# Two transformer blocks on one core: the first weights k-tile by k-tile behind idle products, transposes inside a product, the last tokens tile by tile

## The chip, the core and the metric

One NeuronCore of a Trainium2 chip runs the whole program; the other cores do nothing. The metric is the device time of one execution in microseconds (us), median of 3 runs. TensorE (PE in the profile) multiplies, VectorE (DVE) and ScalarE (ACT) do elementwise work, GpSimd (POOL) a few small operations, SyncE (SP) issues nearly all loads from memory.

## What is computed

256 tokens of width 1024 pass through two blocks. Only the skeleton matters here:

```python
def first_block(x, ...):
    x = x + 0.5 * swiglu(rms_norm(x, ffn1_norm), w_gate, w_up, w_down)        # FFN 1
    x = x + concat(attention(...), pooled(...)) @ w_out                       # first mixer
    x = x + 0.5 * swiglu(rms_norm(x, ffn2_norm), w_gate, w_up, w_down)        # FFN 2

def second_block(x, ...):
    x = x + 0.5 * swiglu_2(rmsnorm(x, ffn1_norm), ...)                        # FFN 3
    x = x + hybrid_mixer(rmsnorm(x, mix_norm), ...)                           # second mixer
    x = x + 0.5 * swiglu_2(rmsnorm(x, ffn2_norm), ...)                        # FFN 4
    return rmsnorm(x, final_norm)
```

`swiglu(h) = (silu(h @ w_gate) * (h @ w_up)) @ w_down`, with 2816 hidden columns. `rms_norm` divides each token by the root of its mean square and multiplies by a gain for each column.

## The kernel before, in words

The tokens are two tiles of 128 (t = 0, 1), kept as `X[t]` (128 x 1024, float32). A product that has to be nearly exact in float32 is made of three products of float32r operands: each operand is split into a high part and a remainder (`split`, lines 63 to 65: ACT copies to `whi`, DVE subtracts to `wlo`), and `mm3` (lines 67 to 72) adds high x high, high x remainder and remainder x high. So 128 tokens times one k-tile (128 rows of a weight) times 512 columns are three PE instructions of 512 columns, on lines 70, 71 and 72.

Weights come in chunks of 128 x 2048 float32 (1 MB), four k-tiles of 512 columns each, through `weights` (lines 53 to 61): a load on SP into one of 3 buffers `raw`, then the two halves of the split into one of 4 buffers `whi` and `wlo`. `rows` (line 94) multiplies a chunk with both token tiles: 24 PE instructions. `feed` (lines 120 to 124) makes the other operand: a k-tile of the transposed tokens times the gain of the norm, split into two parts in `hT`. The norm's division comes later, as a scale `r` from `rstd` (squares by `squares` on ACT, a sum on DVE, a power on POOL).

Each FFN (`ffn`, line 199) works through six column blocks j of gate (G) and up (U); `gated` takes silu(G) on ACT and multiplies with U on DVE, and the transposes of that result are put into `self.late` and done by a `flush` inside a later product. Then two column halves f of the down product (`d`, five chunks of 1 MB and one of 0.5 MB each) are added to X by `add` (line 151), which also takes the squares and, where a norm follows, puts the transposes of X with their `feed` into `self.late` (`pair`).

The start is special: nothing is on the chip yet. `cold_start` (line 178) loads the first chunk of G in four pieces of 256 KB, a piece and its k-tile of the transposed input `xT` at a time, and multiplies it piece by piece: 24 products. The other three chunks of block j = 0 (U, then G, then U again: 72 products) come whole through `weights`, and the tokens `X` themselves are loaded between them.

The first mixer ends with `project` (line 470): four products of mixed tokens with chunks of `w_out`, each for a half of the input and a half f of the columns. The last one is `project(0, 1)`; behind its 24 products `flush` gives PE the transposes of the left half of X, which the first product of FFN 2 needs.

After FFN 4, `run` multiplies X with the last gain, computes `r`, scales on ACT and DVE, and stores four pieces of 256 KB from SP.

The program is written through a tile framework that places the semaphores and, by a model of its own, sets the order of instructions within each engine. Each engine then runs its list in that order.

## Time and profile before

| | us |
|---|---|
| median of 3 runs | 1105.01 |
| lowest, highest | 1104.85, 1106.17 |
| profiled execution: device time | 1106.03 |
| profiled execution: span of the trace | 1104.2 |
| PE busy | 1083.4 |
| DVE busy | 608.8 |
| ACT busy | 506.9 |
| POOL busy | 13.7 |

The profiled execution is 1.0 us slower than the median of the runs, and its own time is 1.8 us more than its span. Times in the trace count from the start of the span. PE is busy nearly all the time, by a modelled end of each pipelined instruction: what PE loses shows as idle time before an instruction, or as a longer distance between the starts of two instructions.

### The profile page before, as it was taken

The page shows a single profiled execution, that of the slowest core. Times are in us where ns is not written, and L with a number is a line of the kernel's source. Part 1 is how long each engine was busy: PE and PEld are TensorE (multiplying, and loading weights), DVE is VectorE, ACT ScalarE, POOL GpSimd, SP SyncE. Part 2 cuts the span into 40 slices and gives each one's busy share as a digit, 9 for nine tenths or more (in the row PEclk, how much of TensorE's full clock was granted, in tenths as well). Part 3 has the DMA queues.
Part 4 walks back from the last instruction along what each step waited for, and adds up shares of the span by engine and source line. Part 5 has one row for each costly group of instructions (what it writes and reads, how often), then busy time and mean ns, then how long its engine had stood idle before and what let it go on. Part 6 is the DMA issues. An engine that isn't in the chain of part 4 may idle for free.

```text
span 1104.2 us, 12761 instructions
## 1 busy us (share of the span) xinstructions
PE 1083.4 (98%) x5250; PEld 907.2 (82%) x5250; DVE 608.8 (55%) x649; ACT 506.9 (46%) x588; POOL 13.7 (1%) x27
## 2 busy tenths in 40 slices
PE   6999999999999999999999999999999999999996
PEld 4888888878788888888888888999888888888885
DVE  4655545698555455445555455687545465545551
ACT  5544434578444444444444444534444345444431
POOL 0000000020000000000000000000000000000000
PEclk8999999999999999999999999999999999999999
DMA  8765544634345554565555455454555555555431
GB/s 305 281 227 191 191 168 150 218 124 171 114 175 191 191 177 174 184 216 211 183 191 191 172 177 200 176 191 157 187 190 191 181 178 178 187 191 187 172 137 39
DMA packets 31739, 201.76 MB, mean 183 GB/s; under 512 B 4545, under 2 KB 4929, under 8 KB 8769
## 3 DMA queue, kind: packets, MB, share of 16 engines
q1 hardware_dynamic: 31680, 200.95, 51.5%
q8 instruction: 41, 0.67, 0.2%
q14 instruction: 18, 0.14, 0.0%
HBM read 199.88 MB, written 1.05 MB: 182 GB/s over the span
## 4 chain that ended last, share of the span: by engine, by line
PE 79%; issue 17%; ACT 1%; DMA 1%; DVE 1%; SPq 0%; POOLq 0%; POOL 0%; ACTq 0%
PE ps L70 25%; PE ps L71 25%; PE ps L72 25%; PE ps L78 2%; PE ps L111 2%; DMA raw<-in_gu 1%; ACT whi L64 1%; DVE wlo L65 1%; PE ps L171 1%; ACT ro L372 0%; PE ps L488 0%; SPq L190 0%; PE ps L384 0%; ACT junk L130 0%; PE ps L318 0%
## 5 line engine op out<-in xcount | busy, mean ns | idle before, releaser
L65 DVE TENSOR_TENSOR wlo<-raw,whi 128x2048 fp32r<-128x2048 f32 (+2 forms) x193 | 425.6, 2206 | 394.4 <-ACT whi L64 394.2
L64 ACT ACTIVATE whi<-raw 128x2048 fp32r<-128x2048 f32 (+2 forms) x193 | 356.1, 1846 | 434.4 <-PE ps L72 315.6
L70 PE MATMUL ps<-whi,hT 128*128 128x512 f32 (+1 forms) x912 | 358.9, 394 | 10.0 <-ACT whi L64 8.5
L71 PE MATMUL ps<-wlo,hT 128*128 128x512 f32 (+1 forms) x912 | 356.0, 390 | 1.6 <-DVE wlo L65 1.6
L72 PE MATMUL ps<-whi,hT 128*128 128x512 f32 (+1 forms) x912 | 355.5, 390 | 0.0
L70 PEld LDWEIGHTS ps<-whi,hT 128*128 128x128 f32 x912 | 172.4, 189 | 45.5 <-ACT whi L64 8.9
L71 PEld LDWEIGHTS ps<-wlo,hT 128*128 128x128 f32 x912 | 172.6, 189 | 36.7 <-DVE wlo L65 2.5
L72 PEld LDWEIGHTS ps<-whi,hT 128*128 128x128 f32 x912 | 172.3, 189 | 35.7
L70 PE MATMUL ps<-whi,act 128*128 128x512 f32 x352 | 138.6, 394 | 0.0
L72 PE MATMUL ps<-whi,act 128*128 128x512 f32 x352 | 138.1, 392 | 0.0
L71 PE MATMUL ps<-wlo,act 128*128 128x512 f32 x352 | 138.0, 392 | 0.0
L72 PEld LDWEIGHTS ps<-whi,act 128*128 128x128 f32 x352 | 66.1, 188 | 14.9
L71 PEld LDWEIGHTS ps<-wlo,act 128*128 128x128 f32 x352 | 66.2, 188 | 14.5
L70 PEld LDWEIGHTS ps<-whi,act 128*128 128x128 f32 x352 | 66.1, 188 | 14.5
L211 ACT ACTIVATE sg<-ps,rstd 128x512 f32<-128x512 f32 (+1 forms) x48 | 31.4, 654 | 64.4 <-PE ps L72 49.5
L70 PE MATMUL ps<-hT,whi 128*128 128x256 f32 x192 | 54.4, 283 | 0.0
L71 PE MATMUL ps<-hT,whi 128*128 128x256 f32 x192 | 54.3, 283 | 0.0
L72 PE MATMUL ps<-hT,wlo 128*128 128x256 f32 x192 | 54.3, 283 | 0.0
L157 DVE SCALAR_TENSOR_TENSOR X<-ps,X 128x512 f32<-128x512 f32 x28 | 19.2, 689 | 44.1 <-PE ps L72 44.1
L213 DVE SCALAR_TENSOR_TENSOR pr<-ps,rstd,sg 128x512 f32<-128x512 f32 (+1 forms) x48 | 33.7, 704 | 12.7 <-PE ps L72 8.5
L71 PEld LDWEIGHTS ps<-hT,whi 128*128 128x128 f32 x192 | 36.9, 192 | 0.0
L70 PEld LDWEIGHTS ps<-hT,whi 128*128 128x128 f32 x192 | 36.9, 192 | 0.0
(152 smaller groups left out, 693.5 us busy)
## 6 DMA issues: line engine op xcount, KB each, us to landing
raw<-in_gu SPq DMA_DIRECT2D x87, 1024.0 KB, 4.8
raw<-in_d SPq DMA_DIRECT2D x40, 1024.0 KB, 4.7
raw<-in_w_out SPq DMA_DIRECT2D x8, 1024.0 KB, 5.0
raw<-in_w_cx SPq DMA_DIRECT2D x8, 1024.0 KB, 4.9
raw<-in_w_v SPq DMA_DIRECT2D x6, 1024.0 KB, 4.9
raw<-in_w_u SPq DMA_DIRECT2D x6, 1024.0 KB, 4.9
raw<-in_de SPq DMA_DIRECT2D x8, 512.0 KB, 3.5
raw<-in_w_b SPq DMA_DIRECT2D x4, 1024.0 KB, 4.9
```

The source lines that it names most:

```text
L64: self.nc.scalar.activation(hi, x, AF.Copy)
L65: self.nc.vector.tensor_tensor(lo, x, hi.bitcast(F32), op=ALU.subtract)
L70: mm(ps, lhsT=a[0], rhs=b[0], start=start, stop=False)
L71: mm(ps, lhsT=a[0], rhs=b[1], start=False, stop=False)
L72: mm(ps, lhsT=a[1], rhs=b[0], start=False, stop=stop)
L78: self.nc.tensor.matmul(ps, lhsT=a, rhs=b, start=start, stop=stop)
L111: self.nc.tensor.transpose(pt[:, i, :], x[t][:, i * P : i * P + P], self.ident)
L157: nc.vector.scalar_tensor_tensor(x, accs[t], scale, x, op0=ALU.mult, op1=ALU.add)
L171: nc.tensor.transpose(pt[:, i, t * P : t * P + P], self.X[t][:, (k + i) * P : (k + i) * P + P], self.ident)
L211: nc.scalar.activation(sg, gs[t], AF.Silu, scale=r[:, t : t + 1])
L213: nc.vector.scalar_tensor_tensor(pr, us[t], r[:, t : t + 1], sg, op0=ALU.mult, op1=ALU.mult)
```

## The change

It has three parts.

The start: `warm_up` gives PE 14 products of a tile of ones with itself, whose result nobody reads. `cold_start` now takes over the whole of block j = 0: all four chunks come in pieces of 256 KB. In the first half (c = 0) each k-tile of G is followed by that of U, in the second (c = 1) the four k-tiles of G come first, then `ident` and X are loaded, then the four of U. `xT` comes in four pieces of two k-tiles. Two loads, `gains` and the first piece of G, are issued by ACT instead of SP, ahead of the load of ACT's table.

```diff
+WARM = 14
...
-    def rows(self, accs, w, x, k0, nk, last, n=512):
+    def rows(self, accs, w, x, k0, nk, last, n=512, tiles=(0, 1)):
-        for t in range(2):
+        for t in tiles:
...
-    def add(self, accs, f, scale, following):
+    def add(self, accs, f, scale, following, tiles=(0, 1)):
-        for t in range(2):
+        for t in tiles:
             x = self.X[t][:, s]
...
-        for t in range(2):
+        for t in tiles:
             self.squares(t, f)
...
+    def warm_up(self):
+        ps = self.ps()
+        for _ in range(WARM):
+            self.mm(ps[:, :P], self.ones, self.ones)
+
     def cold_start(self, accs, src):
-        nc = self.nc
-        raw = self.raw.tile([P, 2048], F32, tag="raw", name="raw")
-        hi = self.wsp.tile([P, 2048], F32R, tag="whi", name="whi")
-        lo = self.wsp.tile([P, 2048], F32R, tag="wlo", name="wlo")
-        xT = self.raw.tile([P, KD, T], F32, tag="raw", name="xT")
+        nc, a = self.nc, self.a
         self.hT = self.big.tile([P, KD, 2, T], F32R, tag="hT", name="hT")
-        for k in range(4):
-            s = slice(k * 512, k * 512 + 512)
-            if k % 2 == 0:
-                nc.sync.dma_start(xT[:, k : k + 2, :], self.a["xT"][:, k : k + 2, :])
-            nc.sync.dma_start(raw[:, s], src[:, s])
-            self.feed(k, xT[:, k, :], "ffn1_norm")
-            self.split(hi[:, s], lo[:, s], raw[:, s])
-            for t in range(2):
-                self.mm3(accs[t], self.both(self.hT[:, k, :, t * P : t * P + P]), (hi[:, s], lo[:, s]), k == 0, False)
-        nc.sync.dma_start(xT[:, 4:8, :], self.a["xT"][:, 4:8, :])
-        for k in range(4, KD):
-            self.feed(k, xT[:, k, :], "ffn1_norm")
+        for c in range(2):
+            w = []
+            for i in range(2):
+                raw = self.raw.tile([P, 2048], F32, tag="raw", name="raw")
+                hi = self.wsp.tile([P, 2048], F32R, tag="whi", name="whi")
+                lo = self.wsp.tile([P, 2048], F32R, tag="wlo", name="wlo")
+                w.append((raw, hi, lo))
+            for i, k in [(i, k) for k in range(4) for i in range(2)] if c == 0 else [(i, k) for i in range(2) for k in range(4)]:
+                kd, s = 4 * c + k, slice(k * 512, k * 512 + 512)
+                raw, hi, lo = w[i]
+                if i == 0 and k % 2 == 0:
+                    xT = self.work.tile([P, 2, T], F32, tag="pr", name="xT", bufs=4)
+                    nc.sync.dma_start(xT, a["xT"][:, kd : kd + 2, :])
+                (nc.scalar if kd + i == 0 else nc.sync).dma_start(raw[:, s], src[i, c][:, s])
+                if kd + i == 0:
+                    first = self.small.tile([P, 1], F32, tag="tot1", name="first")
+                    nc.scalar.activation(first, self.ones[:, :1], AF.Silu)
+                if i == 0:
+                    self.feed(kd, xT[:, k % 2, :], "ffn1_norm")
+                self.split(hi[:, s], lo[:, s], raw[:, s])
+                for t in range(2):
+                    self.mm3(accs[i][t], self.both(self.hT[:, kd, :, t * P : t * P + P]), (hi[:, s], lo[:, s]), kd == 0, kd == KD - 1)
+                if c == 1 and i == 0 and k == 3:
+                    nc.sync.dma_start(self.ident, a["ident"])
+                    for t in range(2):
+                        nc.sync.dma_start(self.X[t], a["x"][t])
+        for t in range(2):
+            for f in range(2):
+                self.squares(t, f)
...
                 if j == 0 and first:
-                    self.cold_start(G, gu[0, 0])
-                else:
-                    self.token_major(G, gu[2 * j], 512, 0)
+                    self.cold_start((G, U), gu)
+                    r = self.rstd()
+                    gated(j, G, U)
+                    continue
+                self.token_major(G, gu[2 * j], 512, 0)
...
+            down = lambda f, c: self.weights(d[f, c] if c < 5 else d_end[f])
             for f in range(2):
                 accs = [self.ps() for _ in range(2)]
-                for c in range(6):
-                    self.rows(accs, self.weights(d[f, c] if c < 5 else d_end[f]), act, 4 * c, 4 if c < 5 else 2, KF - 1)
+                split = f == 1 and following == "final_norm_2"
+                for c in range(4 if split else 6):
+                    self.rows(accs, down(f, c), act, 4 * c, 4 if c < 5 else 2, KF - 1)
                     if c == 0:
                         self.flush()
-                self.add(accs, f, 0.5, following)
+                if split:
+                    ws = [down(f, c) for c in (4, 5)]
+                    for t in range(2):
+                        for c in (4, 5):
+                            self.rows(accs, ws[c - 4], act, 4 * c, 4 if c < 5 else 2, KF - 1, tiles=[t])
+                        self.add(accs, f, 0.5, following, [t])
+                else:
+                    self.add(accs, f, 0.5, following)
...
         def project(half, f):
             accs = [self.ps() for _ in range(2)]
             w = self.weights(a["w_out"][2 * half + f])
-            self.rows(accs, w, mT[half], 0, 4, 3)
-            self.flush()
+            for t in range(2):
+                self.rows(accs, w, mT[half], 0, 4, 3, tiles=[t])
+                self.flush()
             self.add(accs, f, 1.0, None if half else following)
...
-        first = self.small.tile([P, 1], F32, tag="tot1", name="first")
-        nc.scalar.activation(first, self.ones[:, :1], AF.Silu)
-        self.gains = self.load(self.const, "gains", [P, len(NORMS) * KD])
+        self.gains = self.const.tile([P, len(NORMS) * KD], F32, name="gains")
+        nc.scalar.dma_start(self.gains, a["gains"])
         self.ident = self.const.tile([P, P], F32, name="ident")
+        self.warm_up()
...
-        ys = []
-        both = self.raw.tile([P, 2, D], F32, tag="raw", name="y")
         for t in range(2):
-            y = both[:, t, :]
+            y = self.raw.tile([P, 2048], F32, tag="raw", name="y")[:, :D]
+            tot = self.small.tile([P, 1], F32, tag="tot1", name="tot")
+            nc.vector.tensor_tensor(tot, self.sq[:, 0, t : t + 1], self.sq[:, 1, t : t + 1], op=ALU.add)
+            r = self.small.tile([P, 1], F32, tag="r1", name="r1")
+            self.rsqrt(r, tot, 1.0 / D)
             for f in range(2):
                 s = slice(f * 512, f * 512 + 512)
                 nc.vector.tensor_tensor(y[:, s], self.X[t][:, s], self.fg[:, s], op=ALU.mult)
-            ys.append(y)
-        r = self.rstd()
-        for t in range(2):
             for f in range(2):
                 s = slice(f * 512, f * 512 + 512)
                 if f:
-                    nc.vector.tensor_scalar(ys[t][:, s], ys[t][:, s], r[:, t : t + 1], None, op0=ALU.mult)
+                    nc.vector.tensor_scalar(y[:, s], y[:, s], r, None, op0=ALU.mult)
                 else:
-                    nc.scalar.activation(ys[t][:, s], ys[t][:, s], AF.Copy, scale=r[:, t : t + 1])
-                nc.sync.dma_start(self.out[t * P : t * P + P, s], ys[t][:, s])
+                    nc.scalar.activation(y[:, s], y[:, s], AF.Copy, scale=r)
+                (nc.scalar if f == 0 and t == 1 else nc.sync).dma_start(self.out[t * P : t * P + P, s], y[:, s])
```

The first place is SP's list at the start. `xT` is the input, `raw` the weights' buffers (112 and 115 are G and U of the first half, 204 is G of the second), line 190 or 202 a piece, line 57 a whole chunk. Before:

```order
L665 DMA gains_84<-in_gains 128x56
L189 DMA xT_101<-in_xT 128x512
L190 DMA raw_98<-in_gu1 128x512 x2
L189 DMA xT_101<-in_xT 128x512
L190 DMA raw_98<-in_gu1 128x512 x2
L195 DMA xT_101<-in_xT 128x1024
L57 DMA raw_158<-in_gu1 128x2048
L57 DMA raw_188<-in_gu1 128x2048
L231 DMA ident_86<-in_ident 128x128
L233 DMA X0_82<-in_x 128x1024
L233 DMA X1_83<-in_x 128x1024
```
Now:

```order
L201 DMA xT_118<-in_xT 128x512
L202 DMA raw_115<-in_gu1 128x512
L202 DMA raw_112<-in_gu1 128x512
L202 DMA raw_115<-in_gu1 128x512
L201 DMA xT_162<-in_xT 128x512
L202 DMA raw_112<-in_gu1 128x512
L202 DMA raw_115<-in_gu1 128x512
L202 DMA raw_112<-in_gu1 128x512
L202 DMA raw_115<-in_gu1 128x512
L201 DMA xT_210<-in_xT 128x512
L202 DMA raw_204<-in_gu1 128x512 x2
```
`xT` has moved to the head of the list; `gains` and the first piece of G are gone from it, since ACT issues them. Behind these rows stand `ident`, both halves of X, four pieces of U, and from there on whole chunks. From SP's seventh load on each carries a wait for the landing of the load eight places before it (ACT's two counted), since the framework gives out eight completion semaphores in turn; the list of before has such waits too, with fewer and larger loads.

The second place is the end of the first mixer, on PE. `mT` is the mixed tokens, line 171 or 172 a transpose of a piece of X. Before (ps_2301 is the accumulator of the second token tile):

```order
L70 MATMUL ps_2301<-whi_2304,mT_2156 128x512
L71 MATMUL ps_2301<-wlo_2305,mT_2156 128x512
L72 MATMUL ps_2301<-whi_2304,mT_2156 128x512
L171 MATMUL ps_2332<-ident_86,X0_82 128x128
L171 MATMUL ps_2332<-ident_86,X1_83 128x128
```
Now (ps_2346 is the accumulator of the first token tile):

```order
L71 MATMUL ps_2346<-whi_2350,mT_2202 128x512
L72 MATMUL ps_2346<-wlo_2351,mT_2202 128x512
L73 MATMUL ps_2346<-whi_2350,mT_2202 128x512
L172 MATMUL ps_2366<-ident_84,X0_80 128x128
L172 MATMUL ps_2366<-ident_84,X1_81 128x128
```
The eight transposes have moved ahead of the last 12 products. On ACT, `feed` (line 123 or 124) turns their result into `hT`. Before:

```order
L64 ACTIVATE whi_2446<-raw_2444 128x2048
L130 ACTIVATE junk_2297,sq_2294<-X1_83 128x512
L130 ACTIVATE junk_2352,sq_2294<-X0_82 128x512
L64 ACTIVATE whi_2482<-raw_2480 128x2048
L123 ACTIVATE hT_2299<-ps_2332,gains_84 128x256
L123 ACTIVATE hT_2299<-ps_2341,gains_84 128x256
L130 ACTIVATE junk_2354,sq_2294<-X1_83 128x512
```
Now:

```order
L65 ACTIVATE whi_2492<-raw_2490 128x2048
L131 ACTIVATE junk_2343,sq_2340<-X1_81 128x512
L124 ACTIVATE hT_2345<-ps_2366,gains_82 128x256
L124 ACTIVATE hT_2345<-ps_2375,gains_82 128x256
L131 ACTIVATE junk_2398,sq_2340<-X0_80 128x512
L124 ACTIVATE hT_2345<-ps_2366,gains_82 128x256
L65 ACTIVATE whi_2528<-raw_2526 128x2048
L124 ACTIVATE hT_2345<-ps_2375,gains_82 128x256
L131 ACTIVATE junk_2400,sq_2340<-X1_81 128x512
```
Three of the four `feed` rows have moved ahead of the second split of a chunk; the fourth stands behind it.

The third place is DVE's list at the end (line 157 or 158 is `add`, 701 or 729 the product with the last gain, 708 or 733 the last scale). Before:

```order
L157 SCALAR_TENSOR_TENSOR X0_82<-ps_7713,X0_82 128x512
L701 TENSOR_TENSOR y_7890<-X0_82,fg_7148 128x512
L157 SCALAR_TENSOR_TENSOR X1_83<-ps_7714,X1_83 128x512
L701 TENSOR_TENSOR y_7890<-X1_83,fg_7148 128x512
L135 TENSOR_TENSOR tot_7895<-sq_7708 128x2
L84 TENSOR_SCALAR var_7898<-tot_7895 128x2
L708 TENSOR_SCALAR y_7890<-y_7890,rstd_7897 128x512 x2
```
Now:

```order
L158 SCALAR_TENSOR_TENSOR X0_80<-ps_7759,X0_80 128x512
L729 TENSOR_TENSOR y_7936<-X0_80,fg_7194 128x512
L724 TENSOR_TENSOR tot_7937<-sq_7754 128x1
L85 TENSOR_SCALAR var_7940<-tot_7937 128x1
L733 TENSOR_SCALAR y_7936<-y_7936,r1_7939 128x512
L158 SCALAR_TENSOR_TENSOR X1_81<-ps_7760,X1_81 128x512
L729 TENSOR_TENSOR y_7949<-X1_81,fg_7194 128x512
L724 TENSOR_TENSOR tot_7950<-sq_7754 128x1
L85 TENSOR_SCALAR var_7953<-tot_7950 128x1
L733 TENSOR_SCALAR y_7949<-y_7949,r1_7952 128x512
```
The first token tile's chain is complete before the second tile's `add`; on PE the last 18 products are now all of the second tile.

## Rows read from the trace of the kernel before

**Rows 1.** Part 1 of the page: busy time, share of the span, instructions of each engine.
```profile
PE 1083.4 (98%) x5250; PEld 907.2 (82%) x5250; DVE 608.8 (55%) x649; ACT 506.9 (46%) x588; POOL 13.7 (1%) x27
```

**Rows 2.** Waits of PE over the span: total us, times, longest us.
```profile
PE ps L70 <- ACT whi L64: 8.5, 2, 6.4
PE ps L71 <- DVE wlo L65: 1.6, 1, 1.6
PE ps L70 <- ACT hT L123: 1.5, 1, 1.5
```

**Rows 3.** PE by stretch: length, busy us (count), granted clock, DMA share, GB/s.
```profile
6.40:10.70 4.30, 4.29 (x9) 1.00 0.95 342
...
14.50:18.90 4.40, 0.73 (x2) 0.89 0.98 398
18.90:24.60 5.70, 5.67 (x13) 0.50 1.03 364
```

**Rows 4.** Timeline of the start: start us, us, engine, line, instructions.
```profile
0.73 0.20 POOL L675 MEMSET ones<- 128x128 f32 x1 [0.29 <-POOLq L801]
0.74 0.39 SPq L665 DMA_DIRECT2D gains<-in_gains  x1
...
1.18 0.42 SPq L189 DMA_DIRECT2D xT<-in_xT  x1
...
4.93 0.91 ACT L123 ACTIVATE hT<-xT,gains 128x256 fp32r<-128x256 f32 x2 [2.70 <-DMA xT<-in_xT]
...
5.75 1.14 ACT L64 ACTIVATE whi<-raw 128x512 fp32r<-128x512 f32 x2
...
6.41 0.79 PE L70 MATMUL ps<-whi,hT 128*128 128x512 f32 x1 [6.41 <-ACT whi L64]
...
7.14 0.79 PE L71 MATMUL ps<-wlo,hT 128*128 128x512 f32 x1
...
14.64 1.91 ACT L64 ACTIVATE whi<-raw 128x2048 fp32r<-128x2048 f32 x1 [0.75 <-DMA raw<-in_gu]
16.58 2.29 DVE L65 TENSOR_TENSOR wlo<-raw,whi 128x2048 fp32r<-128x2048 f32 x1 [2.17 <-ACT whi L64]
...
24.92 0.39 PE L71 MATMUL ps<-wlo,hT 128*128 128x512 f32 x1
...
43.10 1.03 PE L111 MATMUL ps<-ident,pr 128*128 128x128 f32 x8
```

**Rows 5.** DMA issues, 1.6 to 2.05 us: count, KB each, us to landing.
```profile
xT<-in_xT SPq DMA_DIRECT2D x1, 256.0 KB, 3.7
raw<-in_gu SPq DMA_DIRECT2D x1, 256.0 KB, 3.9
```

**Rows 6.** Timeline of PE at the second mixer's 128x128 f32 products.
```profile
780.87 1.95 PE L78 MATMUL ps<-gv,sgu_w 128*128 128x128 f32 x16
782.57 0.48 PE L70 MATMUL ps<-whi,hT 128*128 128x512 f32 x1
```

**Rows 7.** Timeline around the first mixer's end.
```profile
300.73 1.03 PE L171 MATMUL ps<-ident,X 128*128 128x128 f32 x8
300.93 1.91 ACT L64 ACTIVATE whi<-raw 128x2048 fp32r<-128x2048 f32 x1 [0.93 <-PE ps L72]
...
302.75 0.82 ACT L123 ACTIVATE hT<-ps,gains 128x256 fp32r<-128x256 f32 x2
...
303.26 0.50 PE L70 MATMUL ps<-whi,hT 128*128 128x512 f32 x1 [1.49 <-ACT hT L123]
```

**Rows 8.** Timeline of the end, and us from issue to landing of tile out.
```profile
1095.34 0.39 PE L72 MATMUL ps<-whi,act 128*128 128x512 f32 x1
...
1097.75 0.70 POOL L85 TENSOR_TENSOR rstd<-var,mhalf 128x2 f32<-128x2 f32 x1 [182.04 <-DVE var L84]
...
1098.99 1.81 SPq L711 DMA_DIRECT2D out<-y  x4
...
DMA to landing us min/median/max: 2.1/2.4/2.8
```

More of the change, by code (lines that the diff above doesn't have):

```diff
@@ L229, in ffn @@
                 if j == 0:
-                    if first:
-                        nc.sync.dma_start(self.ident, a["ident"])
-                        for t in range(2):
-                            nc.sync.dma_start(self.X[t], a["x"][t])
-                            for f in range(2):
-                                self.squares(t, f)
                     r = self.rstd()
@@ L701, in run @@
                 nc.vector.tensor_tensor(y[:, s], self.X[t][:, s], self.fg[:, s], op=ALU.mult)
-            ys.append(y)
-        r = self.rstd()
-        for t in range(2):
             for f in range(2):
```

## The prediction

> **What bounds the kernel now.** The first part of the page comes first: PE is busy for 1083.4 of 1104.2 us, every other engine for at most 609 [rows 1]. So only what PE loses can be won, and the list of what PE waits for says where: 8.5 and 1.6 us for the two halves of a weight's split, both within the first 19 us, and once 1.5 us for ACT's `hT` [rows 2]. The table by stretch then shows a loss that is no wait: from 18.9 to 24.6 us the granted clock is 0.50, the 1.2 GHz level, and 13 recorded products fill 5.67 us, 0.43 each [rows 3]. From 6.4 to 10.7 us nine recorded products fill 4.29 us, again at 0.43 or more; the column reads 1.00 there, but the distance is that of the lower level. The timeline gives the full pace: from 24.92 us to the first transposes at 43.10 lie 80 products, 0.227 us each [rows 4]. (Those transposes come after 120 products, the 96 of block j = 0 and 24 of the next, before and after the change alike; so their start measures the whole beginning.) The rest of the span runs at that pace, but for the 1.5 us at the first mixer's end and a tail after the last product.
>
> **The start: when the first products can run.** The first `xT` piece is SP's second load, issued at 1.18 us behind `gains` at 0.74; it takes 3.7 us to land, and ACT's `feed` starts at 4.93 [rows 4, 5]. Now it is SP's first, 0.44 us earlier: it lands at 4.45 and `feed`, 0.46 us (two take 0.91), ends at 5.0. The first piece of G goes out on ACT behind `gains`, at about 1.2 us (0.74 and one issue of 0.4); at 3.9 us to landing [rows 5] it is there at 5.1. Its high half takes 0.57 to 0.65 us (two take 1.14; the first product began 0.66 after the first split) and the first product runs at 5.8; the second needs DVE's remainder and came 0.73 us after the first [rows 4]: 6.5 us. ACT's table load, now behind two issues, is over by 3 us and stays under the wait for `xT`.
>
> From there PE does not wait if pieces come in time. A k-tile of both G and U is 12 products, 2.72 us. ACT needs one `feed` and two splits for it, 0.46 + 2 x 0.57 = 1.6 us, DVE about the same. Quarter splits are dearer than whole ones (4 x 0.57 = 2.28 against 1.91 us [rows 4]), some 1 us more on ACT in all, and that hides under PE as long as PE is the slower. SP issues a piece every 0.47 us, faster than any rate of landing seen. So product 120 is over at 6.5 + 119 x 0.227 = 33.5 us, against 43.10: **9.6 us**. About half of it is the clock (23 or so products at 0.2 us extra), the rest the waits at 14.6 to 18.9 us, where a whole chunk's split (1.91 on ACT, 2.29 on DVE) stood between landing and product.
>
> **The idle products.** They pay only for the clock. Eight products of this shape are 16 rows of the trace and take 1.70 us [rows 6], so 0.2125 each at full clock and 0.425 at half. They can begin at 1.0 us, after `ones` is set [rows 4]. Before, the full pace came 4.3 us after the first product (6.41 to 10.7) and 5.7 us after the second start (18.93 to 24.6) [rows 3, 4]. From 1.0 us that is 5.3 or 6.7 us: ten products at half clock and four at full end at 6.1, or all 14 end by 6.95. The real ones could start at 5.8 and are held by the second at 6.5, so the idle ones cost nothing or 0.45 us. I take **-0.1**, nearer to the first, since that row too starts from a cold chip. The Trainium skill (TensorE: Matmul & The Clock Gate, Part 1: The HAM clock gate) says that the point of release differs from run to run of the same kernel; by it the term would be 0 in some executions and -0.45 in others, which no run here can show yet.
>
> **The loads behind it.** What is late next is the first whole chunk, for j = 1. Up to its landing 7.4 MB must come: 1.05 of `xT`, 4.2 of pieces, 0.07 of `ident`, 1.05 of X, 1.05 of itself. With the queue full the rows show 342, 364 and 398 GB/s [rows 3]; at their mean, 368, the 7.14 MB after the first piece take 19.4 us and are there at 23.9. ACT's 1.91 and DVE's 2.29 bring 28.1, and PE wants the remainder at 6.5 + 96 x 0.227 = 28.3. At 398 there are 1.7 us to spare, at 342 it is 1.3 late. I take **-0.3**. Within the first block each piece has 3 to 4 us to spare at 368. X moves ahead of the last four pieces, and its squares ahead of their splits on ACT: about 3 us of ACT, done near 21 us, before the splits wanted at 22.8 us.
>
> **The first mixer's end.** Before, the transposes run at 300.73, but ACT has a chunk's split before the `feed` (300.93, 1.91 us), `feed` starts at 302.75, and PE waits 1.49 us until 303.26 [rows 7]. Now 12 products, 2.7 us, stand between the transposes and the first use, and three of four `feed` rows stand ahead of that split. X needs DVE's `add` of the product before, whose last instruction is now six products (1.4 us) ahead of the transposes; the `add` takes 0.7. The fourth `feed` still stands behind the split: 0.2 + 1.9 + 0.4 = 2.5 us after the last product of the mixer; the list has it used after 11 products of the next, also 2.5 us. Its remainder comes after DVE's next split, 4.9 us against 22 products, 5.0. So both just fit. Bounds: 1.5 if both do, 0.5 if one is a microsecond late; I take **1.4**.
>
> **The tail.** The last product starts at 1095.34; `add` and squares of both tiles, the sum and POOL's power follow (POOL ends at 1098.45), the scales, and four stores from 1098.99, each 0.45 us after the other, the last landing 2.8 us after its issue near 1100.4: 1103.2, and the span ends 1.0 later [rows 8]. The chain from the last product to POOL's end is the second tile's alone and stays. But the first tile is ahead by 18 products, 4.1 us, and is stored before; so only two stores are left, from two queues, the last issued at about 1099.25. With 2.4 us to landing [rows 8] that is 1101.65: **1.5 us**. Bounds 1.0 (2.8 us to land) and 1.8 (2.1).
>
> **Sum.** 9.6 - 0.1 - 0.3 + 1.4 + 1.5 = 12.1 us off the profiled execution's 1106.03, so 1093.9. That execution is 1.0 above the median of 1105.01: the same sum from there gives **1092.9**. With every bound at its worst, 7.9 + 0.5 + 1.0 = 9.4, so 1095.6; at its best, with the first piece a little earlier as well, 13.2, so 1091.8.
>
> **Rivals.** *The idle products don't release the clock.* Nothing here shows products of ones ahead of real ones. Then they end at 6.95, 0.45 late, and the real ones run 4.3 to 5.7 us at half pace, which loses 2.15 to 2.85: 2.5 to 3.2 beyond the forecast, about 1095.8. For it: two restarts took that long. Against: both ended while PE worked without a gap, and the idle ones work for 5 to 6 us without one. Chance 0.10.
>
> *The pieces come at 300 GB/s.* The queue was only full here with whole chunks among the pieces. Then 7.14 MB take 23.8 us, the first chunk of j = 1 is split at 32.5 instead of 28.3, and 4.2 us go: 1096.8. PE idles between the two blocks, not within the first. Chance 0.12.
>
> *Slower than before: the pieces overlap too little.* If a piece costs 3.9 us whatever else is under way and three are in flight, 0.79 MB come each 3.9 us, 202 GB/s; the chunk for j = 1 is ready at 44.0, 15.7 us late, and the kernel takes about 1108. It decides at 227 GB/s, 3.4 pieces in flight (below that the loss eats all 12.1). Against it: `xT` issued at 1.18 landed at 4.88 and the next piece, issued at 1.65, at 5.55 [rows 4, 5], 256 KB in 0.67 us, six at a time. For it: SP's loads wait for the landing eight places before, and one straggler holds the rest. Chance 0.03. The Trainium skill (DMA: Bandwidth & Descriptors, Anatomy of one DMA - SWDGE (gpsimd) path) speaks for this rival: some 2.0 us fixed for each DMA beside its bytes, on GpSimd's path, hence an estimated 2.6 us for a lone piece; no run here shows a lone piece.
>
> *That the change doesn't do what it says* is left for the clock alone, the first rival: the lists of all engines show the moved steps in their places.
>
> **How the numbers follow.** Forecast within its bounds 0.70, half clock 0.10, 300 GB/s 0.12, too little overlap 0.03, better than the best bound 0.05. The range goes from 1091.0 to 1097.0: the bounds, both middle rivals, and the scatter of about 1 us between runs. A measurement of this kernel tells 0.2%, 2.2 us, from no change. All but the third rival lie below 1102.8: faster 0.95, the same 0.02, slower 0.03.
>
> **What would show it.** Idle products from about 1.0 to 6.1 or 7.0 us; the first real one by 6.5; 0.227 us between real products at once (0.43: first rival); the transposes after 120 products near 33.5 to 34 us; no wait of PE for a split of `raw` over 0.5 us except perhaps at 28 us (over 1.3 there: second rival); no 1.5 us wait at the first mixer's end; two stores after the last product, and 1.5 us less from that product to the end. A wait of PE within the first block, or a clock that falls again there, would make the prediction wrong.

## The result, and the profile after

| | before | changed |
|---|---|---|
| median of 4 runs each, us | 1105.39 | 1094.39 |
| lowest, highest | 1104.85, 1106.17 | 1094.32, 1094.42 |
| profiled execution | 1106.03 | 1094.42 |
| its span | 1104.2 | 1092.6 |

The ratio is 0.990, with a 95% interval from 0.9883 to 0.9917: 11.0 us less by the medians, 11.6 between the two profiled executions. The forecast was 1092.9, or 12.1 less; 1094.4 lies inside the range, 1.5 above the forecast.

Part 1 of the page of the changed kernel, beside [rows 1]: PE does the same work, and 28 rows of idle products, in a shorter span.

```profile
PE 1083.9 (99%) x5278; PEld 909.9 (83%) x5278; DVE 609.7 (56%) x660; ACT 507.6 (46%) x597; POOL 14.1 (1%) x28
```

The waits of PE, beside [rows 2]. The 8.5, 1.6 and 1.5 us there are gone; 1.0 us ahead of the first idle product and 0.2 us for one remainder stand in their place.

```profile
PE ps L79 <- POOL mhalf L703: 1.0, 1, 1.0
PE ps L409 <- ACT ro L397: 0.4, 2, 0.2
PE ps L72 <- DVE wlo L66: 0.2, 1, 0.2
```

The timeline of the start, beside [rows 4]. The idle products fill 0.99 to 6.84 us; ACT's `feed` waits 1.94 us for `gains`, its split 0.66 us for the first piece of G, and the first real product runs at 6.94. From the third on (8.00) they come at full pace, and the transposes behind 120 products start at 34.79 instead of 43.10: 8.31 us earlier.

```profile
0.74 0.41 ACTq L706 DMA_DIRECT2D gains<-in_gains  x1
...
0.99 5.85 PE L79 MATMUL ps<-ones 128*128 128x128 f32 x28 [0.99 <-POOL mhalf L703]
...
1.18 0.45 ACTq L202 DMA_DIRECT2D raw<-in_gu  x1
...
5.09 0.51 ACT L124 ACTIVATE hT<-xT,gains 128x256 fp32r<-128x256 f32 x1 [1.94 <-DMA gains<-in_gains]
...
6.26 1.15 ACT L65 ACTIVATE whi<-raw 128x512 fp32r<-128x512 f32 x2 [0.66 <-DMA raw<-in_gu]
...
6.94 0.50 PE L71 MATMUL ps<-whi,hT 128*128 128x512 f32 x1
...
7.67 0.50 PE L72 MATMUL ps<-wlo,hT 128*128 128x512 f32 x1 [0.22 <-DVE wlo L66]
...
8.00 0.40 PE L73 MATMUL ps<-whi,hT 128*128 128x512 f32 x1
...
34.79 1.03 PE L112 MATMUL ps<-ident,pr 128*128 128x128 f32 x8
```

PE by stretch (length, busy us (count), granted clock, DMA share, GB/s), beside [rows 3]: no gap behind the first products, and the loads move 375 to 415 GB/s. Up to about 15 us these are the pieces of 256 KB and X in two loads of 512 KB; SP issues whole chunks from 15.42 us on.

```profile
5.00:10.00 5.00, 4.68 (x22) 1.00 1.02 380
10.00:15.00 5.00, 5.00 (x24) 1.00 1.05 375
15.00:20.00 5.00, 5.00 (x24) 1.00 1.05 415
20.00:25.00 5.00, 5.00 (x23) 1.00 1.00 394
```

The timeline of the first mixer's end, beside [rows 7]: 12 products of the mixer's own (line 71 and on, operand `mT`) now stand between the transposes and the first product of FFN 2 at 293.43, which waits for nothing.

```profile
289.76 1.04 PE L172 MATMUL ps<-ident,X 128*128 128x128 f32 x8
...
290.98 0.82 ACT L124 ACTIVATE hT<-ps,gains 128x256 fp32r<-128x256 f32 x2
...
293.43 0.40 PE L71 MATMUL ps<-whi,hT 128*128 128x512 f32 x1
```

The timeline of the end, beside [rows 8]: two of SP's three stores go out under the last products; POOL's power, on one column, takes 0.54 us instead of 0.70, and the last store leaves on ACT at 1089.22.

```profile
1084.90 4.42 SPq L736 DMA_DIRECT2D out<-y  x3
...
1085.50 0.39 PE L73 MATMUL ps<-whi,act 128*128 128x512 f32 x1
...
1087.89 0.54 POOL L86 TENSOR_TENSOR r<-var,mhalf 128x1 f32<-128x1 f32 x1 [3.54 <-DVE var L85]
1088.46 0.72 ACT L735 ACTIVATE y<-y,r 128x512 f32<-128x512 f32 x1 [1.03 <-POOL r L86]
```

So the 11.6 us between the profiled executions are: 8.31 up to the first transposes, -0.13 within the first mixer, 1.66 at its end (the following transposes start 9.84 us earlier, and so does the last product), and 1.76 from the last product to the end (8.86 us before, 7.10 now).

### The profile page after: what moved, and what is told of

The parts are those of the page before. It is cut to its first block, busy times and chain, and to the rows that moved or that the text cites. A ratio compares the mean times of both kernels' runs of the same rounds, so it can differ in the third digit from the quotient of the medians.

```text
span 1092.6 us, 12852 instructions
## 1 busy us (share of the span) xinstructions
PE 1083.9 (99%) x5278; PEld 909.9 (83%) x5278; DVE 609.7 (56%) x660; ACT 507.6 (46%) x597; POOL 14.1 (1%) x28
## 4 chain that ended last, share of the span: by engine, by line
PE 96%; DVE 1%; ACT 1%; issue 1%; DMA 0%; POOLq 0%; POOL 0%; ACTq 0%
PE ps L71 30%; PE ps L73 30%; PE ps L72 30%; PE ps L112 2%; PE ps L79 2%; PE ps L172 1%; DMA raw<-in_gu 0%; ACT ro L397 0%; DVE left L373 0%; DVE wlo L66 0%; PE ps L514 0%; ACT whi L65 0%; DVE m L371 0%; ACT rel L360 0%; ACT sqh L389 0%
## 5 line engine op out<-in xcount | busy, mean ns | idle before, releaser
L233 DVE SCALAR_TENSOR_TENSOR pr<-ps,rstd,sg 128x512 f32<-128x512 f32 (+1 forms) x48 | 33.5, 703 | 12.1 <-PE ps L73 7.9
```

The source lines that it names most:

```text
L233: nc.vector.scalar_tensor_tensor(pr, us[t], r[:, t : t + 1], sg, op0=ALU.mult, op1=ALU.mult)
```

## The experiments

They were made on three occasions, each on another chip and with the kernel before beside it: 1105.31 for the first four, 1104.88 for the next four, 1104.53 for the last three. The changed kernel was run anew on the last occasion. From one occasion or execution to another the start moves by up to about 0.9 us (the runs of the last occasion show it), so a part's price is read from its own stretch of the trace, and the medians stand beside it. A trace is one execution.

**No idle products.** What is the clock worth?

```diff
-        self.warm_up()
```

> The change without its 14 idle products; nothing else moves. Clock theory: the idle products pay only for the clock. The first real product starts at 6.9 us as in the change (its split ends there), but it and those behind it run 0.43 us apart until 4.3 to 5.7 us later, the times that the kernel before needed from 6.41 and from 18.93 us. That loses 2.1 to 2.9 us: the 120th product ends at 36.9 to 37.7 instead of 34.8, and the time is 1096.5 to 1097.3. Rival, loads theory: the pieces' landing sets the pace of the first block, so that a slow clock only fills waits that are there anyway; then the 120th product ends within 0.5 us of 34.8 and the time stays at 1094.4 to 1094.9.

Measured: 1095.61 (1094.75 to 1096.68), ratio 0.9915 (0.990 to 0.993), 1.2 us slower than the changed kernel, where 2.1 to 2.9 were expected. PE's timeline shows two reasons: the half pace (0.43 between starts and more) lasts only from 6.51 to 10.4 us, and the first product's piece landed sooner here, so it runs at 6.51 instead of 6.94.

```profile
6.51 0.80 PE L71 MATMUL ps<-whi,hT 128*128 128x512 f32 x1 [6.51 <-ACT whi L65]
...
9.96 0.63 PE L72 MATMUL ps<-wlo,hT 128*128 128x512 f32 x1
10.39 0.51 PE L73 MATMUL ps<-whi,hT 128*128 128x512 f32 x1
10.74 0.39 PE L71 MATMUL ps<-whi,hT 128*128 128x512 f32 x1
...
35.91 1.03 PE L112 MATMUL ps<-ident,pr 128*128 128x128 f32 x8
```

The transposes behind 120 products start at 35.91, 1.12 us later than in the changed kernel's profile (and 0.76 and 1.62 later than in the two experiments that follow, which keep the idle products). From the first product to these transposes it takes 29.40 us against 27.85, so what the clock costs here is 1.55 us. The theory of the clock holds in kind, at a half to three quarters of its price. The other 7.2 us, from 43.10 to 35.91, are the pieces' own between these two traces, whose first products start alike (6.41 and 6.51).

**Transposes behind the mixer's last product again.**

```diff
-            for t in range(2):
-                self.rows(accs, w, mT[half], 0, 4, 3, tiles=[t])
-                self.flush()
+            self.rows(accs, w, mT[half], 0, 4, 3)
+            self.flush()
```

> The change with the transposes behind all 24 products of the first mixer's last product again; start and tail as in the change. Theory: the 1.5 us wait for ACT's hT comes back at that place, as in the kernel before, and nothing else moves: the distance between the two kernels' PE instructions jumps there by the 1.66 us that the change won there, and the time is 1095.9 to 1096.1. Rival: the 1.66 us came with the shifted start (loads and splits fall otherwise against PE from there on), not from the place of the transposes: then PE doesn't wait there and the time stays at 1094.4.

Measured: 1095.99 (1095.25 to 1096.45), ratio 0.9917 (0.9902 to 0.9932): 1.6 us slower, and the wait of [rows 2] is back among PE's waits at its old length. From the transposes behind 120 products to the last product it takes 1.67 us more than the changed kernel. The term for the border is confirmed.

```profile
PE ps L71 <- ACT hT L124: 1.5, 1, 1.5
```

The start of this trace, which the edit doesn't touch, shows two things that the changed kernel's own profile does not. The 14 idle products take 6.23 us, and the first real product, whose split began at 5.42, runs only behind them. And PE waits 0.54 us for the remainder of the first chunk of j = 1.

```profile
0.99 6.23 PE L79 MATMUL ps<-ones 128*128 128x128 f32 x28 [0.99 <-POOL mhalf L702]
...
6.97 0.48 PE L71 MATMUL ps<-whi,hT 128*128 128x512 f32 x1
...
30.02 0.50 PE L72 MATMUL ps<-wlo,hT 128*128 128x512 f32 x1 [0.54 <-DVE wlo L66]
...
35.15 1.03 PE L112 MATMUL ps<-ident,pr 128*128 128x128 f32 x8
...
1087.53 0.39 PE L73 MATMUL ps<-whi,act 128*128 128x512 f32 x1
```

**The old tail.** Both tiles are finished together, with one power and four stores from SP (the functions `run` and `ffn` as they were at these places):

```diff
-                split = f == 1 and following == "final_norm_2"
+                split = False
...
+        r = self.rstd()
...
-                (nc.scalar if f == 0 and t == 1 else nc.sync).dma_start(self.out[t * P : t * P + P, s], y[:, s])
+                nc.sync.dma_start(self.out[t * P : t * P + P, s], ys[t][:, s])
```

> The change with the tail of the kernel before: the last products of both token tiles interleaved by chunk, one root for both tiles, four stores from SP at the end. Theory: what the change won behind the last product (7.1 us from the last product's start to the end of the span, against 8.9) is lost again in full: 1096.1 to 1096.2. Of it 0.2 is POOL's power on one column instead of two, the rest that two stores instead of four stand at the end. Rival: part of it is store traffic that only the second queue saves, or is hidden by the 1 us between the last landing and the end; then less than 1 us is lost.

Measured: 1095.50 (1095.32 to 1095.62), ratio 0.9913 (0.9898 to 0.9928), 1.1 us slower where 1.7 were expected. In the trace the last product starts at 1085.01 and the span ends at 1093.7: a tail of 8.69 us against 7.10, so 1.6 us. The missing 0.5 us is the start's: here the first loads landed sooner than in the changed kernel's profile, and the transposes behind 120 products start at 34.29 instead of 34.79.

```profile
34.29 1.03 PE L112 MATMUL ps<-ident,pr 128*128 128x128 f32 x8
...
1085.01 0.39 PE L73 MATMUL ps<-whi,act 128*128 128x512 f32 x1
```

**Idle products in the kernel before.** Is the clock a gain by itself?

```diff
+        self.warm_up()
```

> The kernel before with nothing but the 14 idle products ahead. Theory: idle products and loads in pieces only pay together. The clock is free when the first real products start (about 6.9 us), and the 24 of the first chunk end near 12.4 instead of 14.3 us, but the next chunk still lands at 14.6 us and PE waits for its split as before; so the 120th product ends within 0.3 us of 43.1 and the time is 1105.0 to 1105.7. It may even be longer, if the longer idle time brings the clock down earlier. Rival: the gains add up; the 2 us that the clock cost ahead of 10.7 us are won whole, the time is 1103.2 to 1103.6.

Measured: 1105.35 (1104.03 to 1106.43), ratio 1.0002 (0.9992 to 1.0011): nothing by the medians, to within about 1 us. The first products come at full pace, reach the whole chunk's split sooner and wait there; the clock then falls once more, as in [rows 3] (0.50 granted from 16.3 to 18.6 us), and the half pace lasts to about 22.4 us. In the one trace the transposes behind 120 products still start at 41.90, 1.2 us ahead of the kernel before, where at most 0.3 were expected; the runs of this kernel scatter over 2.4 us and those of the kernel before over 1.3, so the single traces decide nothing against ten and thirteen runs. In this kernel, then, idle products pay clearly only where PE does not run dry behind them.

```profile
16.34 1.22 PE L70 MATMUL ps<-whi,hT 128*128 128x512 f32 x2 [3.34 <-ACT whi L64]
18.67 0.80 PE L71 MATMUL ps<-wlo,hT 128*128 128x512 f32 x1 [1.10 <-DVE wlo L65]
...
41.90 1.03 PE L111 MATMUL ps<-ident,pr 128*128 128x128 f32 x8
```

**The first piece of G on SP.** It took 5.1 us from its issue on ACT to its landing, where 3.9 were forecast: is it the second queue?

```diff
-                (nc.scalar if kd + i == 0 else nc.sync).dma_start(raw[:, s], src[i, c][:, s])
+                nc.sync.dma_start(raw[:, s], src[i, c][:, s])
```

> The change with the first piece of G issued by SP right behind xT instead of by ACT behind gains (gains stay on ACT); 14 idle products. In the change that piece needed 5.1 us to land, at 6.3 us, where 3.9 were forecast; the pieces that SP issued at the same time were moved beside it. Queue theory: two queues share the engines, so what ACT issues waits for SP's later pieces; on SP the piece is ahead of them and lands at 5.1 to 5.5 us. The scheduler now puts two feeds ahead of the first split, so the split starts at about 5.8 to 6.0 and the first real product could run at 6.5 but waits for the idle ones (6.2 to 6.9); the second follows within 0.4 instead of 0.7 us. The time falls by 0.2 to 0.6 us, to 1093.8 to 1094.2. Rival: the memory side is slow at the start whatever the queue, the piece lands at 6.2 again, and the time is that of the change, 1094.4, or longer by the second feed (0.5).

Measured: 1095.70 (1095.40 to 1096.79), ratio 0.9918 (0.9905 to 0.9932). A miss: the start is even earlier than expected (first product 5.97, not 6.2 to 6.9), and still the kernel is slower than expected by 1.5 to 1.9 us. The next two kernels move the start further.

**11 idle products** in the kernel just described:

```diff
-WARM = 14
+WARM = 11
```

> As the one before with 11 idle products, which end at 5.6 us at half clock. If the queue theory holds, the first real product starts at 6.5 at the latest, free of the idle ones; the clock comes at any time from 5 to 8 us, and what is late costs half of it. Theory: 0.1 to 0.4 us less than with 14, about 1093.7, with a wider scatter from run to run. Rival: the three idle products missing move the release of the clock behind the first real products more often, which costs up to 0.8 us: 1094.4 to 1095.0.

Measured: 1095.23 (1095.05 to 1095.51), ratio 0.9912 (0.9899 to 0.9926); first product 5.86. A miss in the same way.

**The first k-tile of the input alone**, on top of both:

```diff
-                    nc.sync.dma_start(xT, a["xT"][:, kd : kd + 2, :])
+                    n = 1 if kd == 0 else 2
+                    nc.sync.dma_start(xT[:, :n, :], a["xT"][:, kd : kd + n, :])
+                elif i == 0 and kd == 1:
+                    nc.sync.dma_start(xT[:, 1:2, :], a["xT"][:, 1:2, :])
```

> As the one before, and the first load of xT holds one k-tile instead of two (128 KB instead of 256), its other half behind the first pieces of G and U. Theory: the chain to the first product is landing of xT, feed, split. xT lands 0.3 us earlier, G's piece too, and one feed instead of two stands ahead of the split: the first real product at 5.6 to 6.0 us, and the time 1093.0 to 1093.6. Rival: gains, on ACT, land at 5.0 us in any case (4.3 us in the change) and hold the feed; then the first product is at 6.2 and the gain against the one before is 0.3 at most.

Measured: 1095.22 (1094.40 to 1095.38), ratio 0.9911 (0.9898 to 0.9925). A miss as well. The halved load lands 2.5 us after its issue, the first product runs at 5.01, 1.93 us ahead of the changed kernel's, and nothing of it is left at the second block's transposes (57.63 against 57.45). The timelines of PE and DVE at the border of blocks j = 0 and j = 1 show where it goes:

```profile
27.06 1.43 DVE L236 SCALAR_TENSOR_TENSOR pr<-ps,rstd,sg 128x512 f32<-128x512 f32 x2 [2.57 <-PE ps L73]
27.93 1.28 PE L112 MATMUL ps<-ident,pr 128*128 128x128 f32 x8
28.41 2.28 DVE L66 TENSOR_TENSOR wlo<-raw,whi 128x2048 fp32r<-128x2048 f32 x1
30.74 0.50 PE L72 MATMUL ps<-wlo,hT 128*128 128x512 f32 x1 [1.54 <-DVE wlo L66]
...
57.63 1.03 PE L112 MATMUL ps<-ident,pr 128*128 128x128 f32 x8
```

The high half of the first chunk of j = 1 is done at 26.07 here (ACT, 24.16 and 1.91 long). But in DVE's list the two products with U (`pr`) now stand ahead of that chunk's remainder, and wait until 27.06 for PE's last sums; the remainder comes at 28.41, and PE waits 1.54 us for it. On PE the transposes follow two products of j = 1 instead of 24, and from their start to the next product it takes 2.81 us instead of 0.79 (34.79 to 35.58 in the changed kernel): that is about the whole gain. In the changed kernel DVE has the remainder first:

```profile
26.63 2.29 DVE L66 TENSOR_TENSOR wlo<-raw,whi 128x2048 fp32r<-128x2048 f32 x1 [3.78 <-ACT whi L65]
28.93 1.41 DVE L233 SCALAR_TENSOR_TENSOR pr<-ps,rstd,sg 128x512 f32<-128x512 f32 x2
```

The same 1.54 us stand in the traces of the two kernels before this one (at 31.63 and 31.54 us). The framework turned the two around when the loads at the head of the program were moved; no line of the program says so.

**The second half of block j = 0 in whole chunks.**

```diff
-                (nc.scalar if kd + i == 0 else nc.sync).dma_start(raw[:, s], src[i, c][:, s])
+                if c == 0:
+                    (nc.scalar if kd + i == 0 else nc.sync).dma_start(raw[:, s], src[i, c][:, s])
+                elif k == 0:
+                    nc.sync.dma_start(raw, src[i, c])
...
-                self.split(hi[:, s], lo[:, s], raw[:, s])
+                if c == 0:
+                    self.split(hi[:, s], lo[:, s], raw[:, s])
+                elif k == 0:
+                    self.split(hi, lo, raw)
```

> The change with the second half of the first block (G and U of k-tiles 4 to 7) loaded and split as whole chunks of 1 MB again; the first half stays in pieces. Theory: by then the loads are ahead of PE. G's chunk lands near 14.8 us, its split ends at 16.7 on ACT and 19.0 on DVE, and PE wants the remainder at 18.6; U's chunk lands near 19.6 and is split by 23.9, wanted at 24.0. So 0.2 to 0.8 us are lost: 1094.6 to 1095.2. Rival: whole chunks bring back the waits that the kernel before had at that place (2.1 us for the high half, 1.6 for the remainder): 1097 to 1098.

Measured: 1094.65 (1094.56 to 1095.07), ratio 0.9908 (0.9894 to 0.9921), with one wait in the block:

```profile
18.75 0.50 PE L72 MATMUL ps<-wlo,hT 128*128 128x512 f32 x1 [0.66 <-DVE wlo L66]
```

The remainder of U's chunk is a little late too: the first product with it starts at 24.56, 0.69 us after the first of the two ahead of it, where 0.45 is the pace. From the first product to the transposes it takes 29.00 us, against 27.85 and 27.86 in the two traces of the changed kernel. So the pieces of the second half are worth about 1.15 us, more than the one wait and the 0.2 to 0.8 of the theory; the time came out inside the forecast because the start was earlier here (first product 6.16, against 6.94). The rival of 1097 to 1098 falls: it is in the first half that the pieces win most of their 7.2 us.

```profile
6.16 0.48 PE L71 MATMUL ps<-whi,hT 128*128 128x512 f32 x1
...
35.16 1.03 PE L112 MATMUL ps<-ident,pr 128*128 128x128 f32 x8
```

**The changed kernel again, and two that keep its lists with the earlier start.** Both have the early start of the kernel with the halved load (first piece of G on SP, 11 idle products, first k-tile alone). The first of the two gives the first chunk of j = 1 in four pieces, so that its remainders stand ahead of `pr` on DVE:

```diff
+                    early = self.quarters(gu[2, 0])
                     gated(j, G, U)
                     continue
-                self.token_major(G, gu[2 * j], 512, 0)
+                if j == 1 and first:
+                    self.rows(G, early, self.hT, 0, 4, KD - 1)
+                else:
+                    self.token_major(G, gu[2 * j], 512, 0)
...
+    def quarters(self, src):
...
+        for k in range(4):
+            s = slice(k * 512, k * 512 + 512)
+            self.nc.sync.dma_start(raw[:, s], src[:, s])
+            self.split(hi[:, s], lo[:, s], raw[:, s])
```

The second leaves that chunk whole and loads and splits it ahead of `ident`, X and the squares:

```diff
-                if c == 1 and i == 0 and k == 3:
-                    nc.sync.dma_start(self.ident, a["ident"])
-                    for t in range(2):
-                        nc.sync.dma_start(self.X[t], a["x"][t])
...
+                    early = self.weights(gu[2, 0])
+                    nc.sync.dma_start(self.ident, a["ident"])
+                    for t in range(2):
+                        nc.sync.dma_start(self.X[t], a["x"][t])
```

> The changed kernel itself, as the control for the two kernels beside it. If its time on another chip is what it was: 1094.2 to 1094.7, first real product at 6.5 to 7.0 us, transposes after 120 products at 34.4 to 34.9. If the moments at which the first loads land and the clock is released scatter as the earlier profiles say, the first real product may stand anywhere from 6.2 to 7.2.

> The start of e7_half_xT (first k-tile of the input alone, first piece of G on SP, 11 idle products), and the first chunk of j = 1 in four pieces too, so that DVE has all four remainders ahead of the two products with U. Theory (what e7 won at its first product, 1.9 us, was given back by one order of DVE's list, 1.5 us, and nothing else): no wait of PE over 0.3 us at 27 to 32 us, transposes after 120 products at 32.7 to 33.3, last product 1083.5 to 1084.0, time 1092.3 to 1093.1. Rival (the list gives it back at another place, or an earlier start takes a landing that comes no earlier): a wait of 1 to 2 us elsewhere in the first 60 us, time 1094.2 to 1095.2.

> The same start, and the first chunk of j = 1 whole but loaded and split ahead of ident, X and the squares, with its remainder ahead of the products with U on DVE. Theory as for e10_quarters: no wait of PE over 0.3 us at 27 to 32 us, transposes after 24 products of j = 1 at 32.7 to 33.3, time 1092.3 to 1093.1. Rival (X, now 1 MB later, makes the squares, the scale and so the transposes late): PE waits 0.5 to 2 us at 32 to 34 us for the gated product, time 1093.2 to 1095.0.

| | us | runs | ratio to before | first product | transposes after 120 products |
|---|---|---|---|---|---|
| changed kernel again | 1093.59 | 1093.54 to 1093.89 | 0.9902 (0.9887 to 0.9916) | 6.07 | 33.93 |
| chunk in four pieces | 1092.61 | 1092.47 to 1092.98 | 0.9893 (0.9878 to 0.9907) | 5.31 | 33.47 |
| chunk before X | 1092.80 | 1092.41 to 1093.13 | 0.9893 (0.9876 to 0.9909) | 5.71 | 33.67 |

With the list mended, the earlier start stays: PE has no wait over 0.3 us behind the first products in either kernel, the transposes are back behind 24 products of j = 1, and both are faster than the changed kernel, by 1.0 and 0.8 us, each of their runs below each of its runs. The rivals fall, though the transposes come at 33.47 and 33.67, not at the 32.7 to 33.3 of the theory. The gain is less than the 1.9 us won at the first product of the earlier kernel's profile: the changed kernel itself starts 0.87 us sooner here (and at 1093.59 lies below the 1094.2 to 1094.7 expected of it), and the two new kernels' first products come 0.30 and 0.70 later than in that profile. In the traces 0.46 and 0.26 us of the gain stand at the transposes, and 0.64 and 0.41 at the last product (1084.66, against 1084.02 and 1084.25); the rest of the medians' 1.0 and 0.8 isn't accounted for, and both profiled executions are the slowest of their four. DVE's timeline of the kernel with four pieces has the remainders ahead of `pr`:

```profile
26.36 1.90 DVE L76 TENSOR_TENSOR wlo<-raw,whi 128x512 fp32r<-128x512 f32 x3 [0.24 <-ACT whi L75]
28.17 1.40 DVE L246 SCALAR_TENSOR_TENSOR pr<-ps,rstd,sg 128x512 f32<-128x512 f32 x2
```

And the start of the changed kernel on this occasion, beside the one shown above:

```profile
0.99 5.22 PE L79 MATMUL ps<-ones 128*128 128x128 f32 x28 [0.99 <-POOL mhalf L703]
...
5.39 1.15 ACT L65 ACTIVATE whi<-raw 128x512 fp32r<-128x512 f32 x2 [0.75 <-DMA raw<-in_gu]
...
6.07 0.50 PE L71 MATMUL ps<-whi,hT 128*128 128x512 f32 x1
...
33.93 1.03 PE L112 MATMUL ps<-ident,pr 128*128 128x128 f32 x8
```

The first piece of G, still on ACT, is split from 5.39, against 6.26 before; on SP it was 5.29. So the theory of the queue falls: the same load on ACT took 5.1 us to land in the first profile and 4.1 to 4.6 in the five other traces that have it there, on SP 4.0 and 4.1 in two. Why the first profile's was the latest stays open. The first product moves by 0.87, the transposes by 0.86 and the profiled time by 0.82 us with it.

## Why the prediction was right, and where its terms were off

- **The start, 9.6 forecast.** Right in mechanism: pieces in time, full pace from the third product on, no wait within the block but 0.22 us for the first remainder. The step that was off is "at 3.9 us to landing it is there at 5.1": the piece took 5.1 us and was there at 6.26, so the first product ran at 6.94, not 5.8, and the second at 7.67, not 6.5. In the other traces with this load on ACT it took 4.1 to 4.6, so 3.9 was short in all of them. On the last occasion, at 4.2 us to landing, the second product ran at 6.80 and the transposes came at 33.93, inside the "33.5 to 34" of the forecast.
- **The idle products, -0.1.** They took 5.85 us, 0.209 for each of 28 rows, half clock all through. In this profile they cost nothing, since the first piece was later than they were. In the trace of the experiment with the transposes moved back they did: they took 6.23 us, and the third real product came at 7.53, 2.11 after its split began (5.42), against 1.74 in the second trace of the changed kernel (7.13 and 5.39). So both cases of the prediction, nothing and about 0.45, occur. What they are worth is 1.55 us by the trace and 1.2 by the medians, where the rival on the clock put 2.5 to 3.2. That price had 0.45 us for a delay by the idle products themselves, and half pace for 4.3 to 5.7 us; the half pace lasted 3.9 us in the kernel without them, and for its first 0.7 the second product waits for its remainder at either level. The Trainium skill (TensorE: Matmul & The Clock Gate, Part 1: The HAM clock gate) says that the point of release differs from run to run of one kernel. The traces agree: the same 14 products took 5.85 and 5.22 us in two executions of the changed kernel, 4.84 in that with the old tail, and the 6.23 above.
- **The loads behind, -0.3.** Not needed in the two traces of the changed kernel; in the trace with the 6.23 us above, which has the same loads, PE did wait 0.54 us at that place. From 5 to 25 us 375 to 415 GB/s came, against 342 to 398 in [rows 3]; the remainder of the next block's first chunk was done at 28.92 (26.63 and 2.29 long), and PE's products of it began at 29.34, the first with the remainder at 29.80. Both rivals on the loads fall. The Trainium skill (DMA: Bandwidth & Descriptors, Anatomy of one DMA - SWDGE (gpsimd) path) puts some 2.0 us fixed beside each DMA's bytes, on GpSimd's path. Here the loads go out from SP and ACT: a first piece took 2.9 to 5.1 us, but with a queue full of them no fixed part showed in the rate.
- **The mixer's end, 1.4.** 1.66 by the trace, 1.6 by the runs with it undone: the upper bound, 1.5, was a little low. The product that waited had cost 1.49 us of idle time; what makes up the rest wasn't shown.
- **The tail, 1.5.** 1.76 by the trace, within the bounds. Beyond the forecast came a shorter power (0.54 instead of 0.70).
- **What no term had**: 0.13 us more within the first mixer. Its cause stays open; the traces of the last two kernels are 0.15 to 0.18 us shorter again in that mixer.

8.31 - 0.13 + 1.66 + 1.76 = 11.60, against 1106.03 - 1094.42 = 11.61. The forecast of 12.1 was 0.5 too much: 0.9 at the start and 0.13 in the first mixer, of which the mixer's end and the tail gave back 0.26 each: that the sum came so close is in part luck. The other 1.0 of the 1.5 us between 1092.9 and 1094.39 is the base. All terms were read from a profiled execution that lay 1.0 above the median of 1105.01, and were then taken off that median; the changed kernel's profiled execution lies on its own (1094.42 and 1094.39). The range held.

## What to carry to other kernels

A gain at the head of a program is real only if the next thing is not late by as much: idle products won 1.2 us where the pieces behind them were ready, and nothing by the medians in the kernel before, where PE ran into a split. Where a framework sets the order, compare the lists of all engines after every edit, however far from the edit: two rows exchanged on DVE at 28 us gave back all that an earlier first load had won at 5 us. And time the kernel that is to be improved again beside each attempt: the changed kernel's own start moved by 0.9 us from one occasion to the next.

## What was not expected

- The time from issue to landing of the first loads differs by execution: 4.1, 4.3 and 5.1 us (first input, `gains`, first piece of G) in the first profile of the changed kernel, 3.2, 3.4 and 4.2 in the second, and 3.1 to 3.4, 3.3 to 3.6 and 4.1 to 4.6 in the four others with the same first loads. With a first load of half the size (128 KB) all three came sooner, 2.5, 2.7 and 2.9 to 3.2 us, in three kernels. Why the smaller load also hastens the piece behind it was not tried.
- `gains`, only 28 KB, landed 1.8 us after its issue on SP in the kernel before, and 2.7 to 4.3 us on ACT beside the first input. It, and no longer the input, released the first `feed`. Ahead of everything on SP it was not tried in the changed kernel.
- The granted clock reads 1.00 in the stretch of the idle products, although their distance, 0.209 us for a row where [rows 6] have 0.106 (1.70 us for 16), is that of the lower level. At the head of the trace the distance of the starts tells the clock, and the column does not:

```profile
0.90:6.90 6.00, 5.85 (x28) 1.00 0.76 264
6.90:11.00 4.10, 3.84 (x16) 1.00 1.03 370
```
